# A one-core trunk layer: the feed-forward weights' sums moved in 64 long rows, loads issued one step before their use, and a rearranged last half

## The chip, the cores and the metric

The kernel runs on one core of a Trainium2 chip. The metric is the device time in microseconds, as the median of several runs. A profile shows one execution: PE is TensorE, ACT is ScalarE, DVE is VectorE, POOL is GpSimd, SP is SyncE, whose queue issues most of the DMAs.

## The reference

One layer of a streaming encoder, batch 1, 2048 frames, width 1024, 16 heads of 64, all in float32. x is the residual stream; g are gains.

```python
def rms_norm(x, g):
    return x * rsqrt(mean(x * x, axis=-1) + 1e-6) * g

# DEPTH = 1, mixer 0
h = rms_norm(x, g_pre_mix)
m = chunk_relpos_attention(h, w_qkv, w_o, rel_bias)
#   frame chunk c (64 frames) attends to chunks max(0, c-8)..c:
#   softmax(q k^T / 8 + bias[clipped relative position]) v, then @ w_o
x = x + rms_norm(m, g_post_mix)
h = rms_norm(x, g_pre_ffn)
x = x + rms_norm((silu(h @ w_gate) * (h @ w_up)) @ w_down, g_post_ffn)   # inner width 2816
```

## The kernel before

Activations lie transposed, features on the 128 partitions and frames along the rows, in halves of 512 frames; two halves are a group (`g` = 0, 1). Each float32 factor of a dense product is split into a high and a low part (`split`: ACT writes the high part, DVE the rest), and `products` issues three matmuls (high·high, high·low, low·high). One such triple of 512 columns is the unit of `tick`.

PE's order is written out by hand: `dense()` is a generator of PE's work, and the main loop takes pieces of it between the attention steps (`fill`). The instructions of the other engines are put in order by the tile framework's scheduler, which issues what its own model holds ready, by buffers and data; on the chip each engine then runs its list strictly in order. Work that lies beside the products waits in the list `later` as pairs of a cost and a step; `tick` adds the products done to a credit and runs the steps that it pays for. `pause(w)` is an empty step of cost w.

Attention runs first, for both groups. Each of 64 steps a group is: `scores` (PE products L555, DVE takes the bias and the maximum L564, ACT the exponential L568, POOL multiplies by the reciprocal of the sums L572), then `transposed` (PE transposes of the scores L588 and L599, DVE and ACT copy them out L591, L593, L600), and once in four steps `output`. PE cannot transpose scores that POOL has not scaled.

The feed-forward products use a scheme of seven block products in place of eight. It needs four sums of weight blocks, S1 to S4, for each of 11 column blocks of the gate and up weights (512 KB a block) and of the down weights (256 KB): 22 units. [...] S2 adds S1, and S4 adds S2. [...] The sums' tiles hold the column block in the middle, `[128, 11, 1024]`, so a transfer has 128 rows of 4 KB or 2 KB. The kernel asks for a small area for the descriptors of POOL's DMAs:

```python
    nc = bacc.Bacc("TRN2", target_bir_lowering=False, num_devices=1, dynamic_dma_scratch_size=512)
```

Buffers that matter here: `io` has 3 buffers of 512 columns; `narrow` takes turns over 9 (4 of the tag `sc`, 5 of `tmp` once the feed-forward phase has begun); `big` is one buffer of 10 × 512 columns, used by `Blocks.first` for the third columns' sources and then by `gate_up` for its terms (`p1`, `p5`, `u2`).

`Blocks` makes the normalised and combined columns of the feed-forward input: `sums` (squares), `spreads` (roots to rows), `column` (load and normalise), `first`, `second`, `third` for group 0 and `all` for group 1. `Late` is the norm and residual addition of a half whose product was left in DRAM: `sums`, `rstd`, `write`. In group 0 of the gate and up products, `later` holds the two halves' `Late` of group 1's attention, then `blocks[1].sums`. `gate_up` ends a block product in `closing` (DVE L980, ACT's sigmoid-linear unit L982).

The last stage is `down` for group 1. Its last product goes in two halves of 256 columns; `keep` stores a part (DVE L1075), squares it (ACT L243) and adds the squares (DVE L244). `rstd_steps` brings the squares' sum to PE (L258), takes mean and power on DVE and POOL (L260, L262), transposes the roots to rows (PE L274) and copies them out (ACT L275). `finish` multiplies (L1375), adds the residual (L1376) and stores, all additions on DVE; pieces of two columns for the first 256 frames, of four for the second. `Post.finish` does the same for the other half of the group and gives half of its additions to POOL (L392).

Of the kernel before, what the change touches and what calls it, by code (L numbers as in the profile page):

```python
# [50 lines left out]
def trunk(  # L51
# [45 lines left out]
    sum_gu = {n: dram.tile([P, NF // 2, 1024], F32, name=f"gu_{n}") for n in ("S1", "S2", "S3", "S4")}  # L97
    sum_d = {n: dram.tile([P, NF // 2, HALF], F32, name=f"d_{n}") for n in ("S1", "S2", "S3", "S4")}
# [114 lines left out]

    def pause(w):
        return [(w, lambda: None)]
# [30 lines left out]
    def rstd_steps(total, dst, wait=8.0, keep=None, bank=None):  # L246
# [8 lines left out]
        def by_token():  # L255
            pt = bank("pssq")
            for b in range(nb):
                pe.matmul(pt[:, 0, b : b + 1], total[:, b * P : b * P + P], ones[:, 0:1], start=True, stop=True)  # L258
# [5 lines left out]
        return [(1.0, by_token)] + pause(wait) + [(1.0, lambda: spread(r[0], dst, bank))]  # L264
# [4 lines left out]
    def spread(r, dst, bank=norm_bank):  # L269

        pt = bank("prs")
        nb = dst.shape[-1] // P
        for b in range(nb):
            pe.transpose(pt[:, b, :], r[:, b : b + 1].to_broadcast([P, P]), ident)  # L274
        act.activation(dst, pt[:, :nb, :].rearrange("p b t -> p (b t)"), AF.Copy)  # L275
# [92 lines left out]
    class Post:  # L368
# [31 lines left out]
        def write(self, w=1.6):  # L400
            def one(dt):
                def go():
                    y = self.y[dt]
                    n = y.shape[-1]
                    io = xp.tile([P, HALF], F32, tag="io", name="res", bufs=3)[:, :n]
                    sp.dma_start(io, self.res[:, dt, :])
                    dve.scalar_tensor_tensor(
                        y, y, gt[:, self.gain, dt : dt + 1], self.total, op0=ALU.mult, op1=ALU.mult
                    )
                    dve.tensor_tensor(y, io, y, op=ALU.add)  # L410
                    sp.dma_start(self.dst[:, dt, :], y)

                return w, go

            return [one(dt) for dt in range(KT)]
# [308 lines left out]
    class Blocks:  # L724
# [9 lines left out]
        def sums(self, w):  # L734

            steps = []
            for t in range(2):
                def one(k, t=t):
                    if k == 0:
                        self.total = nrm_tile("total")  # L740
                    c = io("sum")
                    sp.dma_start(c, self.src[t][:, k, :])
                    add_square(c, self.total, k == 0)

                steps += [(w, lambda k=k, one=one: one(k)) for k in range(KT)]
# [13 lines left out]
        def column(self, dst, t, k):  # L759
            sp.dma_start(dst, self.src[t][:, k, :])  # L760
            dve.scalar_tensor_tensor(
# [8 lines left out]
        def first(self, w):  # L770
# [3 lines left out]
            def load(k):  # L774
# [3 lines left out]
                c[k] = [io("b11"), io("b12"), io("b22")]  # L778
                for dst, t, kk in zip(c[k], (0, 1, 1), (k, k, k + 4)):
                    self.column(dst, t, kk)  # L780
                self.column(self.wait[:, 4 + k, :], 0, k + 4)

            def sums(k):
                b11, b12, b22 = c[k]
# [9 lines left out]

            for k in range(4):
                steps += [(w, lambda k=k, f=f: f(k)) for f in (load, sums, put)]
            return steps

        def all(self, w):
# [3 lines left out]
            def load(k):  # L803
                c[k] = [io("b11"), io("b12"), io("b22"), narrow("b21")]
                for dst, t, kk in zip(c[k], (0, 1, 1, 0), (k, k, k + 4, k + 4)):
                    self.column(dst, t, kk)

            def one(k):
                b11, b12, b22, b21 = c[k]
# [22 lines left out]
        def second(self, w):  # L832
            def one(k, name, t):
                c = io("b2")
                self.column(c, t, k + 4)
                self.put(name, k, c)

            return [(w, lambda k=k, n=n, t=t: one(k, n, t)) for n, t in (("B21", 0), ("B22", 1)) for k in range(4)]
# [709 lines left out]
```

## Time and profile before

| what | value |
|---|---|
| median of 3 runs | 2446.33 us |
| runs | 2441.12, 2446.33, 2449.23 us |
| profiled execution | 2441.91 us |
| its span, first to last instruction | 2440.1 us |
| granted TensorE clock, mean | 0.996 |
| PE busy | 2399.6 us (98%) |
| DVE, ACT, POOL busy | 1468.8, 1030.7, 302.6 us |
| DMA moved | 488.41 MB, 200 GB/s on average |

The span is divided about so: attention with the projections to 1153 us, gate and up products of group 0 from there, then its down products, and the same for group 1 to the end. In a table of windows the columns are the stretch, its length, the busy time of each engine (with instructions), the granted clock, the busy share of the 16 DMA engines and GB/s. A row of waits gives who waited for whom, the sum, how often, and the longest. A row of the timeline gives start, duration, engine, line and operation, and in brackets the idle time before it and what ended it.

### The profile page before, as it was taken

Reading aid. Unit: us, or ns where it says so; the run is one execution under the profiler, and the core shown is the slowest. Engines: PE = TensorE matmul, PEld = TensorE weight load, DVE = VectorE, ACT = ScalarE, POOL = GpSimd, SP = SyncE. Lnnn points to the kernel's source line nnn. Section 1 sums busy time; section 2 is a strip of 40 time slices with the busy share of each in tenths; the row PEclk is TensorE's granted clock in tenths of the full one; section 3 lists DMA queues with packets and bytes.
Section 4 is the critical chain, followed back from the end, with each engine's and each line's share of the span. In section 5 each row is a group of like instructions: output and inputs, shape, how many; then the busy total and the mean of one; then the engine's idle time right before and its main releaser. Section 6 shows DMA issues by size and latency. Waiting matters only on the chain.

```text
span 2440.1 us, 34891 instructions
## 1 busy us (share of the span) xinstructions
PE 2399.6 (98%) x12554; PEld 1993.0 (82%) x12554; DVE 1468.8 (60%) x2569; ACT 1030.7 (42%) x1807; POOL 302.6 (12%) x379
## 2 busy tenths in 40 slices
PE   9999999999999999999999999999999999999997
PEld 8887878788888888878888788888888888888886
DVE  6555455767555554667566665577666655555577
ACT  5444334654344443545333333365443333334444
POOL 0233233201233332210000000000000000000001
PEclk9999999999999999999999999999999999999999
DMA  7689888757898975546476755377667655457654
GB/s 219 196 216 234 221 229 203 222 183 200 226 250 214 243 182 133 144 143 225 157 252 201 242 171 170 123 246 256 210 214 246 219 178 160 135 170 243 195 188 147
DMA packets 209884, 488.41 MB, mean 200 GB/s; under 512 B 25360, under 2 KB 27424, under 8 KB 208432
## 3 DMA queue, kind: packets, MB, share of 16 engines
q1 hardware_dynamic: 197040, 451.59, 58.3%
q0 software_dynamic: 12672, 34.61, 9.3%
q8 instruction: 99, 1.62, 0.3%
q14 instruction: 73, 0.60, 0.1%
HBM read 356.54 MB, written 148.42 MB: 207 GB/s over the span
## 4 chain that ended last, share of the span: by engine, by line
PE 48%; DMA 4%; DVE 3%; issue 1%; ACT 0%; SPq 0%; DVEq 0%; ACTq 0%
PE pd L192 6%; PE pd L193 6%; PE pd L194 6%; PE pb L192 4%; PE pb L193 4%; PE pb L194 4%; PE pa L192 3%; PE pa L193 3%; PE pa L194 3%; PE pc L192 3%; PE pc L194 3%; PE pc L193 3%; DMA b<-x 1%; DMA res<-in_x 1%; DMA y<-y 1%
## 5 line engine op out<-in xcount | busy, mean ns | idle before, releaser
L568 ACT ACTIVATE sc<-sc,nmax 128x640 f32<-128x640 f32 (+4 forms) x256 | 193.1, 756 | 277.5 <-DVE nmax L564 276.7
L192 PE MATMUL mm<-hb,whi 128*128 128x512 f32 x704 | 290.0, 412 | 0.5 <-ACT y L239 0.5
L194 PE MATMUL mm<-hb,wlo 128*128 128x512 f32 x704 | 277.0, 393 | 0.0
L193 PE MATMUL mm<-hb,whi 128*128 128x512 f32 x704 | 276.1, 392 | 0.0
L572 POOL TENSOR_SCALAR sc<-sc,rows 128x640 f32<-128x640 f32 (+4 forms) x256 | 198.6, 813 | 438.4 <-DVE rows L571 418.7
L564 DVE CUSTOM_DVE_ANT_0 sc<-st,bias 128x640 f32<-128x640 f32 (+4 forms) x256 | 179.6, 738 | 100.2 <-PE st L556 94.9
L192 PE MATMUL pb<-hb,whi_gu_T 128*128 128x512 f32 x528 | 206.9, 392 | 4.8 <-DVE terms L980 4.8
L194 PE MATMUL pb<-hb,wlo_gu_T 128*128 128x512 f32 x528 | 206.0, 390 | 0.0
L193 PE MATMUL pb<-hb,whi_gu_T 128*128 128x512 f32 x528 | 205.9, 390 | 0.0
L262 POOL TENSOR_TENSOR rs<-ms,neg_half 128x4 f32<-128x4 f32 (+1 forms) x11 | 16.7, 1520 | 1248.1 <-DVE ms L260 1248.1
L192 PEld LDWEIGHTS mm<-hb,whi 128*128 128x128 f32 x704 | 132.9, 189 | 35.2 <-issue 14.7
L194 PEld LDWEIGHTS mm<-hb,wlo 128*128 128x128 f32 x704 | 132.4, 188 | 29.4
L193 PEld LDWEIGHTS mm<-hb,whi 128*128 128x128 f32 x704 | 133.1, 189 | 19.4
L193 PE MATMUL pd<-a,whi_d_T 128*128 128x512 f32 (+1 forms) x368 | 139.9, 380 | 0.4 <-DVE a L348 0.4
L192 PE MATMUL pd<-a,whi_d_T 128*128 128x512 f32 (+1 forms) x368 | 140.0, 381 | 0.0
L194 PE MATMUL pd<-a,wlo_d_T 128*128 128x512 f32 (+1 forms) x368 | 139.7, 380 | 0.0
L192 PE MATMUL pa<-hb,whi_gu_B 128*128 128x512 f32 x352 | 137.7, 391 | 0.5 <-ACT terms L961 0.5
L193 PE MATMUL pa<-hb,whi_gu_B 128*128 128x512 f32 x352 | 137.0, 389 | 0.0
L194 PE MATMUL pa<-hb,wlo_gu_B 128*128 128x512 f32 x352 | 137.0, 389 | 0.0
L192 PE MATMUL mm<-whi,hb 128*128 128x256 f32 x448 | 133.5, 298 | 0.0
L555 PE MATMUL st<-k,q 128*128 128x384 f32 (+1 forms) x448 | 131.9, 315 | 0.2 <-DVE nmax L564 0.2
L129 DVE TENSOR_TENSOR wlo_gu_T<-raw,whi_gu_T 128x1024 fp32r<-128x1024 f32 x88 | 107.4, 1221 | 40.5 <-ACT whi_gu_T L128 40.3
(219 smaller groups left out, 5642.8 us busy)
## 6 DMA issues: line engine op xcount, KB each, us to landing
raw<-gu_S SPq DMA_DIRECT2D x88, 512.0 KB, 3.9
raw<-in_w_gu SPq DMA_DIRECT2D x66, 512.0 KB, 4.1
q<-stage SPq DMA_DIRECT2D x128, 256.0 KB, 5.8
y<-y SPq DMA_DIRECT2D x96, 256.0 KB, 3.8
gu_S<-in_w_gu SPq DMA_DIRECT2D x44, 512.0 KB, 7.6
raw_a<-aT SPq DMA_DIRECT2D x88, 256.0 KB, 3.6
raw_d<-d_S SPq DMA_DIRECT2D x88, 256.0 KB, 3.6
raw<-in_w_a SPq DMA_DIRECT2D x42, 512.0 KB, 6.3
```

The source lines that it names most:

```text
L129: dve.tensor_tensor(lo, raw, hi.bitcast(F32), op=ALU.subtract)
L192: pe.matmul(pt, a_hi, b_hi, start=first, stop=False, skip_group_check=go_on)
L193: pe.matmul(pt, a_hi, b_lo, start=False, stop=False, skip_group_check=go_on)
L194: pe.matmul(pt, a_lo, b_hi, start=False, stop=last, skip_group_check=go_on)
L262: pool.tensor_tensor(r[0][:, :nb], m[:, :nb], neg_half.to_broadcast([P, nb]), op=ALU.pow)
L555: pe.matmul(st[:, a:b], q[:, 2 * h, cols], kk[:, h, key], start=True, stop=False)
L564: dve.tensor_tensor_reduce(out=sc[:, :n], in0=st[:, c0 : c0 + n], in1=rev, scale=-1.0, scalar=3.0e38, op0=ALU.add, op1=ALU.min, accum_out= ...
L568: act.activation(sc[:, :n], sc[:, :n], AF.Exp, bias=nmax, scale=-1.0, accum_out=rows[:, 0:1])
L572: last_pool[0] = pool.tensor_scalar(sc[:, :n], sc[:, :n], rows[:, 1:2], 1.0, op0=ALU.mult, op1=ALU.mult)
```

## The change

Five things are edited.

1. `weight_sums`: the sums' tiles and the down weights lie with the column block outermost, so that a block is contiguous; copies and adds are seen as 64 rows of twice the length (`long`, at most 8192 bytes a row). The order of the copies and adds over the steps is a new one: gate-and-up units and down units take turns, a unit's copies go out every second step, and its adds 4, 8, 10 and 14 steps after its first copy (before: 5, 6, 8, 11).
2. A helper `behind` makes steps in which the load of step k goes out with the use of step k − lag. `Post.write`, `Blocks.sums`, `Blocks.second`, `Late.sums` and `Late.write` use it; `Blocks.first` and `Blocks.all` issue their loads in a step of their own, ahead of the normalising (`norm`, now apart from `column`). `Late.write` holds `y` in a `narrow` buffer, and `first` and `second` take `io` and `narrow` buffers by turns.
3. `Blocks.third` of group 0 is run from `later` beside the first products, not ahead of them; the pause after it is 44 instead of 56, and one of 12 is put ahead of `blocks[1].sums`. The first `p1` pair of `gate_up` lies in `narrow` buffers.
4. In the last half the last column's squares stay in a tile of their own and go to PE as a second term of the sum; the roots' rows stay in PSUM and are read there by DVE; POOL makes one addition of the first 256 frames and two of the second; all pieces have two columns.
5. The pause ahead of the other half's norm is 6 instead of 4.

```diff
-    sum_gu = {n: dram.tile([P, NF // 2, 1024], F32, name=f"gu_{n}") for n in ("S1", "S2", "S3", "S4")}
-    sum_d = {n: dram.tile([P, NF // 2, HALF], F32, name=f"d_{n}") for n in ("S1", "S2", "S3", "S4")}
+    sum_gu = {n: dram.tile([NF // 2, P, 1024], F32, name=f"gu_{n}") for n in ("S1", "S2", "S3", "S4")}
+    sum_d = {n: dram.tile([NF // 2, P, HALF], F32, name=f"d_{n}") for n in ("S1", "S2", "S3", "S4")}
...
+    def behind(w, n, lag, load, use):
+        def one(k):
+            def go():
+                if k < n:
+                    load(k)
+                if k >= lag:
+                    use(k - lag)
+            return w * n / (n + lag), go
+        return [one(k) for k in range(n + lag)]
...
     def weight_sums():
+        def long(t):
+            return t.rearrange("(a b) c -> a (b c)", b=2)
         def copy(to, a):
             with tc.issue_after(last_sp[0].ins):
-                sp.dma_start(to, a)
+                last_sp[0] = nc.sync.dma_start(long(to), long(a), max_dma_last_dim=8192)
         def add(to, a):
             with tc.issue_after(last_pool[0].ins):
-                pool.dma_start(to, a, accum_op=ALU.add)
+                pool.dma_start(long(to), long(a), accum_op=ALU.add, max_dma_last_dim=8192)
         steps = [[] for _ in range(4 * len(units) + 8)]
         for u, (src, dst) in enumerate(units):
+            at = 8 * (u // 2) + u % 2
             for n, (to, a) in enumerate((("S1", "A21"), ("S3", "A11"), ("S2", "A11"), ("S4", "A12"))):
-                steps[4 * u + n].append((copy, dst[to], src[a]))
-            for n, to, a in ((5, "S1", src["A22"]), (6, "S3", src["A21"]), (8, "S2", dst["S1"]), (11, "S4", dst["S2"])):
-                steps[4 * u + n].append((add, dst[to], a))
+                steps[at + 2 * n].append((copy, dst[to], src[a]))
+            for n, to, a in ((2, "S1", src["A22"]), (4, "S2", dst["S1"]), (5, "S3", src["A21"]), (7, "S4", dst["S2"])):
+                steps[at + 2 * n].append((add, dst[to], a))
...
     class Late:
         def write(self, w):
-            def one(dt):
-                y, res = io("y"), io("res")
+            c = {}
+            def load(dt):
+                c[dt] = y, res = narrow("y"), io("res")
                 sp.dma_start(y, self.y[:, dt, :])
                 sp.dma_start(res, self.res[:, dt, :])
+            def use(dt):
+                y, res = c.pop(dt)
                 dve.scalar_tensor_tensor(
                     y, y, gt[:, self.gain, dt : dt + 1], self.total, op0=ALU.mult, op1=ALU.mult
                 )
                 dve.tensor_tensor(y, res, y, op=ALU.add)
                 sp.dma_start(self.dst[:, dt, :], y)
-            return [(w, lambda dt=dt: one(dt)) for dt in range(KT)]
+            return behind(w, KT, 1, load, use)
...
+            if (g, c) == (0, 0):
+                p1 = [narrow("p1") for _ in range(2)]
...
-        for step in blocks[0].third(0.0):
-            step[1]()
         for g in range(NG):
             i = 2 * g
             if g == 0:
-                later.extend(pause(56.0))
+                later.extend(blocks[0].third(1.5) + pause(44.0))
                 for t in range(2):
                     late = Late(y_d[t], POST_MIX, x[2 + t], x1_d[2 + t])
                     later.extend(late.sums(6.0) + late.rstd(6.0) + late.write(10.0))
-                later.extend(blocks[1].sums(8.0) + blocks[1].spreads())
+                later.extend(pause(12.0) + blocks[1].sums(8.0) + blocks[1].spreads())
...
             def keep(t, dt, here, put):
                 put(y[t][:, dt, here])
-                add_square(y[t][:, dt, here], total[t][:, here], t not in begun)
+                if t == 0 and dt == KT - 1:
+                    last_sq[here.start] = narrow("sq")[:, : here.stop - here.start]
+                    act.activation(last_sq[here.start], y[t][:, dt, here], AF.Square)
+                else:
+                    add_square(y[t][:, dt, here], total[t][:, here], t not in begun)
...
-            def finish(here, per):
+            def finish(r, here, n):
...
-                def one(k):
-                    a, b_ = (v[:, k : k + per, here] for v in (y[0], res[0]))
+                def one(k, eng):
+                    a, b_ = (v[:, k : k + 2, here] for v in (y[0], res[0]))
                     dve.tensor_tensor(a, a, r, op=ALU.mult)
-                    dve.tensor_tensor(b_, b_, a, op=ALU.add)
-                    sp.dma_start(out[i][:, k : k + per, here], b_)
-                return [(0.0, lambda k=k: one(k)) for k in range(0, KT, per)]
+                    eng.tensor_tensor(b_, b_, a, op=ALU.add)
+                    sp.dma_start(out[i][:, k : k + 2, here], b_)
+                return [lambda k=k: one(k, pool if k < KT - 2 * n else dve) for k in range(0, KT, 2)]
...
-                    later.extend(pause(4.0) + rstd_steps(post.total, post.total, 5.0) + post.finish(2.0, 2))
+                    later.extend(pause(6.0) + rstd_steps(post.total, post.total, 5.0) + post.finish(2.0, 2))
```

More of the change, by code (lines that the diff above doesn't have):

```diff
@@ L793, in put @@
                     self.put(name, k, src)
+            order = [(load, 0)]
             for k in range(4):
-                steps += [(w, lambda k=k, f=f: f(k)) for f in (load, sums, put)]
-            return steps
+                order += [(load, k + 1), (sums, k), (put, k)]
+            return steps + [(w, lambda k=k, f=f: f(k)) for f, k in order if k < 4]
         def all(self, w):
@@ L832, in second, with load, use @@
         def second(self, w):
[L833 to L838, printed above, removed]
+            c = {}
+            def load(n):
+                c[n] = (io, narrow)[n % 2]("b2")
+                self.column(c[n], n // 4, n % 4 + 4)
+            def use(n):
+                self.norm(c[n], n // 4, n % 4 + 4)
+                self.put(("B21", "B22")[n // 4], n % 4, c.pop(n))
+            return behind(w, 8, 2, load, use)
         def third(self, w):
@@ L1151, in one @@
                 sp.dma_start(self.dst[:, dt, :], y)
-            return [(w, lambda dt=dt: one(dt)) for dt in range(KT)]
+            return behind(w, KT, 1, load, use)
     def begin():
```

122 lines of the change are left out of this document (78 added, 44 removed).

## The prediction

> **What bounds the kernel now.** I read the page's busy times first: they say whether there is an engine whose work is the time, or waits.
>
> ```profile
> PE 2399.6 (98%) x12554; PEld 1993.0 (82%) x12554; DVE 1468.8 (60%) x2569; ACT 1030.7 (42%) x1807; POOL 302.6 (12%) x379
> ```
>
> TensorE is busy for 2399.6 of 2440.1 us. No part of the change takes a product away, so all it can win is the 40.5 us in which PE idles, and what PE loses at a lower clock. The windows say where the idle time lies (second column: PE busy; before the DMA share: granted clock), and PE's waits say who ends it (total, times, longest).
>
> ```profile
> 244.00:305.00 61.00, 56.53 (x387) 49.22 (x385) 27.66 (x76) 23.80 (x57) 17.54 (x24) 0.97 0.86 221
> 305.00:366.00 61.00, 55.20 (x295) 42.83 (x294) 31.13 (x76) 21.83 (x49) 20.59 (x27) 0.97 0.89 229
> 2379.00:2440.00 61.00, 47.28 (x255) 40.41 (x253) 43.17 (x71) 27.95 (x52) 10.08 (x5) 0.91 0.42 148
> ```
>
> ```profile
> PE tt L588 <- POOL sc L572: 8.2, 3, 4.7
> PE tt L599 <- DVE pT L591: 5.8, 8, 1.5
> PE pb L192 <- DVE terms L980: 4.8, 3, 3.1
> PE pssq L258 <- DVE total L244: 3.2, 3, 2.1
> PE pa L192 <- ACT terms L961: 0.5, 1, 0.5
> ```
>
> So 10.3 us of idle lie in 122 us of attention, 13.7 us in the last 61 us, and the rest is small. Three sites answer to three parts of the change.
>
> **Part 1, the weights' sums.** 88 adding transfers go out from POOL's queue (L868), one per score step, between the scalings of the scores (L572) for which PE waits. Look at one of them:
>
> ```profile
> q0 software_dynamic: 12672, 34.61, 9.3%
> 341.08 0.85 POOL L868 DMA_DIRECT2D gu_S<-gu_S  x1 [6.10 <-DVE nmax L564]
> 341.68 1.43 POOL L572 TENSOR_SCALAR sc<-sc,rows 128x384 f32<-128x384 f32 x2
> 351.36 0.87 POOL L868 DMA_DIRECT2D d_S<-d_S  x1 [8.25 <-issue]
> DMA to landing us min/median/max: 10.0/10.0/10.0
> 353.01 1.77 PE L588 MATMUL tt<-ident,sc 128*128 128x128 f32 x8 [4.66 <-POOL sc L572]
> POOL d_S L868 <- issue: 103.3, 28, 8.2
> POOL gu_S L868 <- issue: 47.7, 21, 6.8
> 268.22:271.63 3.41, 3.41 (x19) 3.41 (x18) 0.42 (x1) 0.43 (x1) 0.00 (x0) 0.50 0.86 245
> 353.55:356.96 3.41, 3.41 (x12) 2.81 (x11) 1.45 (x3) 1.11 (x2) 0.28 (x2) 0.50 0.51 79
> ```
>
> The landing line is that of the transfer issued at 341.08: it lands at 341.08 + 10.0 = 351.1. The next leaves POOL at 351.36, after 8.25 us in which POOL waited for nothing that the profile shows. Its data was not what it waited for: these two work on different tensors. The two scalings behind it on POOL wait with it, and PE waits 4.66 us for them. 49 issues waited in this way, 151 us in all. I read this as room for one transfer's packets and no more. 12672 packets over 88 transfers are 144 each, which is 16 × 9: on each of 16 DMA engines eight of a transfer's 128 rows and one more. With 64 rows it is 4 + 1 = 5. A room that holds nine and not eighteen holds two of five if it is ten or more; three if it is fifteen or more. Then POOL waits only for the transfer before the last, one score step earlier, and a landing of 10.0 us is covered by two steps (the two issues above are 10.3 us apart and were stretched by the wait itself).
>
> What goes: PE's 8.2 us, and the two half-clock stretches that follow the stalls (3.41 us each at 0.50, PE busy throughout: half of each is lost, 1.7 us, 3.4 together). **11.6 us.** Bounds: nothing, if the room was just nine or POOL sends adding transfers one by one; 13.5 us, if a third of the 5.8 us of L599 waits goes too. What is late next there is DVE's copy L591, which is in that row already. The longer order of copies and adds moves SP's 88 copies by up to three steps; each stays one a step, and the adds stay behind their copies by four steps or more (five before for the first, three between two adds, now four), so no wait for data is added. The weights' new order in memory leaves the SBUF loads at 128 rows: nothing.
>
> **Part 2, loads a step ahead.** The clearest site is where the first half's late norm ends and `blocks[1].sums` begins:
>
> ```profile
> 1361.82 5.35 DMA x<-y
> 1367.19 3.18 DMA sum<-x
> 1370.45 0.63 ACT L239 ACTIVATE total<-sum 128x512 f32<-128x512 f32 x1 [10.63 <-DMA sum<-x]
> 1377.55:1380.96 3.41, 2.94 (x7) 2.36 (x8) 3.06 (x5) 1.58 (x2) 0.00 (x0) 0.50 0.88 250
> DVE y L1147 <- DMA y<-y: 38.0, 19, 3.9
> ```
>
> The first two rows are of the chain that ended last (start, duration, what). The `sum` tile takes an `io` buffer that the last `y` held; it is free only when `y` is stored (5.35 us); then it is loaded (3.18 us); and ScalarE, in order, sits 10.63 us before the square of it, with the split of the next weights and the sigmoid of `terms` queued behind. PE pays the 3.1 us of the `pb` row and half of 2.94 us at clock 0.50, 1.5 us. With the change `y` lies in a `narrow` buffer, `res` alone takes one of three `io` buffers and frees it at DVE's addition, and a pause of 12 stands between: the wait on the store is gone, 4.6 us. The other 1.7 us of the `pb` row follow DVE's own waits for late `y` loads (38.0 us in all, 3.9 at most); a load one step of 10 × 8/9 = 8.9 credits ahead should cover 3.9 us, but these additions also stand in a queue of splits, so I take half, 0.8. **5.4 us**, bounds 0 and 6.3 (4.8 + 1.5).
>
> The same edit elsewhere (`Post.write`, `Blocks.first`, `all`, `second`, both `sums`) moves loads on SP's queue and the normalising on DVE's by one step, in stretches where PE has no wait in the rows above: cost nothing now, hidden by DVE's 40% idle time. If that cover fails, the price is one stall like the longest of PE's, 4.66 us, with 1.7 us of half clock. An SP load that now waits for a `narrow` buffer holds up the weights' loads queued behind it; those are asked for four products ahead, so that I expect no PE wait of it. For all the redrawn orders of DVE, ACT and SP together I take a loss of **2 us**, between 0 and one such stall, 6.4.
>
> **Part 3, small edits.** The third columns' splits move from in front of the first products to beside them, and the first `p1` pair lies outside the `big` buffer that these splits hold: the 0.5 us of the `pa` row goes; bounds 0 and 0.5, and −1 for two splits too many on ACT in front of a copy. A pause of 6 instead of 4 ahead of the second-last norm: of the `pssq` row all but the longest is 1.1 us; half goes. Together **1.0 us**.
>
> **Part 4, the end.**
>
> ```profile
> 2426.53 0.60 DVE hb L1375
> 2427.12 0.35 DVE total L244
> 2427.61 0.59 PE pssq L258 x4
> 2428.53 1.07 POOL L262 TENSOR_TENSOR rs<-ms,neg_half 128x2 f32<-128x2 f32 x1 [6.35 <-DVE ms L260]
> 2430.39 0.38 ACT L275 ACTIVATE total<-prs 128x256 f32<-128x256 f32 x1 [2.87 <-PE prs L274]
> 2428.45 1.20 DVE hb L1375 x2
> 2429.65 1.21 DVE hb L1376 x2
> 2430.86 2.31 DVE hb L1375 x2
> 2433.16 1.14 DVE hb L1376
> out_dram<-hb SPq DMA_DIRECT2D x6, 512.0 KB, 3.0
> out_dram<-hb SPq DMA_DIRECT2D x4, 256.0 KB, 2.2
> L392 POOL TENSOR_TENSOR hb<-hb,hb x4: 1285/2212/5346, 2375.4 to 2390.8; 128x512 f32<-128x512 f32 x4
> L389 DVE SCALAR_TENSOR_TENSOR hb<-hb,gt,total x8: 739/742/1789, 2371.3 to 2385.3; 128x512 f32<-128x512 f32 x8
> ```
>
> DVE works without a break from the first half's multiplications to the end, and the second half's roots arrive (2430.39 + 0.38) just as it gets free, so both must shrink. Roots: the last square goes to PE as a second term: L244 (0.35 and a hop, 0.45 us) goes, two more products of 0.15 us each come behind the square; the copy L275 and its hop (0.45) go, since DVE reads the bank: 0.45 − 0.3 + 0.45 = 0.6 us earlier. DVE: of what stands in front of the second half one addition (0.6) goes to POOL and one L244 (0.35) goes altogether, 0.95 us, so DVE is free by then. Second half: 4 multiplications and 2 additions at 0.6 us are 3.6 us, against 2.31 + 2 × 1.14 = 4.6 now; that is if POOL's two additions cost DVE nothing. If POOL and DVE shut each other out, 3.6 + 2 × 1.285 = 6.2. The L389 row has a median near its minimum and one at 1.789: most operations beside POOL's ran unslowed, so I stay nearer the lower bound, at 4.4: 0.2 us won. The last transfer is 256 KB instead of 512 KB: 0.8. **1.6 us**, bounds −0.2 (6.2) and 2.4 (3.6).
>
> [...] The 1.789 us row agrees with an exclusion; no row here shows a PSUM input beside POOL.
>
> **Sum.** 11.6 + 5.4 + 1.0 + 1.6 − 2 = 17.6 us off the profiled execution's 2441.9 us (span 2440.1). The median of the runs, 2446.33, is 4.4 us above that execution; taken off the median, the time is 2428.7 us.
>
> **Rivals.**
> (a) POOL still sends one at a time (the room is nine, or it is no matter of room). For it: in no place do two overlap, so the trace can't tell these apart. Against: nothing but the code's halved rows. Then 11.6 us stay: 17.6 − 11.6 = 6.0, 2440.3 us.
> (b) The loads come no earlier, because SP issues them when a buffer is free and not when the step says so. For it: the 5.35 us store in front of the `sum` load is a buffer's wait. Against: the change also moves `y` to other buffers. 12.2 us, 2434.1.
> (c) Slower: the long rows make DMA the bound in attention. Place: 127 to 427 us, where the sums run.
>
> ```profile
> 127.00:427.00 300.00, 289.52 (x1865) 243.93 (x1865) 152.85 (x387) 118.92 (x273) 93.94 (x127) 0.99 0.88 222
> raw<-in_w_o SPq DMA_DIRECT2D x20, 512.0 KB, 5.3
> raw<-in_w_o SPq DMA_DIRECT2D x6, 1024.0 KB, 4.9
> ```
>
> The share of the 16 engines there is 0.88. POOL's 9.3% of the span is 227 us of all engines, and nearly half of its transfers (41 of 88 would be 106 us) fall in these 300 us, a share of 0.35. It decides once these packets take over a third more time per byte (0.35 × 0.34 = 0.12). At twice the time the share would be 1.23 and the stretch 69 us longer; with the 6.0 us of the other parts, 2446.3 + 69 − 6 = 2509 us; at a half more, 0.88 + 0.175 = 1.055, 16 us and 2456 us. Against it: a row twice as long (1024 KB over 128 rows) lands in 4.9 us where the shorter takes 5.3.
> (d) At the end POOL and DVE exclude each other throughout (6.2 us instead of 4.4), and the pow of the second roots stands behind a POOL addition of 1.285 us: 17.6 − 1.8 − 1.3 = 14.5, 2431.8 us. For it the 5346 ns of one L392 row; against it the three shorter ones.
>
> **How the numbers follow.** The forecast as it stands 0.50; (a) 0.18; (b) 0.11; (c) 0.05; (d) 0.11; some other new stall that eats most of the gain 0.05. About 0.3% (7.3 us) is what a measurement here can tell from no change: the runs before spread over 2441.12 to 2449.23. So faster means under 2439.0: the forecast, (b), (d) and four tenths of (a), 0.79; same: the rest of (a) and most of the other stall, 0.15; slower: (c) and the rest, 0.06. The likeliest case's own range is 2421 (13.5 + 6.3 + 1.6 + 2.4 = 23.8 with no loss, 2422.5, and somewhat less for the runs' spread) to 2435 (the loss of 6.4 in full, and a little). The range over the cases is 2420 to 2443: (a) with the spread of a run, and not (c).
>
> **What would show it.** Part 1: POOL's waits put down to "issue" fall from 151 us to under 20, two transfers overlap, the `tt L588` row falls under 2 us, and no half-clock stretch is left near 268 or 353 us; if POOL's issues still follow a landing by 0.3 us, (a) holds. Part 2: no ACT row with 10 us of idle time before `total<-sum`; the `pb` row under 2 us; `y L1147 <- DMA y<-y` far below 38 us, else (b). Part 4: from the last product to the end of the span some 13 us instead of 14.6; L392-like POOL rows over 2 us, or DVE additions over 1 us, speak for (d). DMA share above 0.95 with longer landings of the weights speaks for (c). The prediction is wrong as a whole if PE's idle time stays near 40 us, or if it falls and matmuls get longer.

## The result, and the profile after

The changed kernel takes 2416.16 us (median of 4, 2415.36 to 2416.70) against 2443.72 us (2441.12 to 2449.23) for the kernel before in the same comparison: a ratio of 0.9878, interval 0.9854 to 0.9902. The forecast, 2428.7, had the right sign and about two thirds of the size (17.6 us off the median, 27.6 measured); the time lies below its range. The profiled execution takes 2415.77 us (span 2414.0, clock 0.998), 26.1 us less than the one before, where the prediction's sum was 17.6.

Busy time of the engines and POOL's DMA queue, from the page of the changed kernel:

```profile
PE 2392.5 (99%) x12562; PEld 1991.0 (82%) x12562; DVE 1462.7 (61%) x2568; ACT 1031.3 (43%) x1805; POOL 294.7 (12%) x382
q0 software_dynamic: 5632, 34.61, 8.7%
```

PE's idle time went from 40.5 to 21.5 us (span less busy), and its busy time fell by 7.1 us although it multiplies the same matrices. The queue moves the same 34.61 MB in 5632 packets instead of 12672. That is 64 a transfer on average, where the prediction reckoned 16 × 5 = 80 for all of them: 44 × 16 × 5 and 44 × 16 × 3 make the 5632. In the trace the queue's packets are 4224 of 8192 bytes and 16 of 4 bytes a transfer: only the 512 KB blocks go as 64 rows, the 256 KB blocks as 32, three packets an engine with the small one. The first two windows shown before, the last 61 us of the span, and the waits of PE (a choice of rows):

```profile
244.00:305.00 61.00, 61.00 (x421) 53.26 (x420) 28.79 (x79) 24.94 (x59) 18.77 (x27) 1.00 0.94 262
305.00:366.00 61.00, 61.00 (x388) 51.41 (x386) 34.08 (x92) 26.11 (x60) 20.38 (x30) 1.00 0.94 245
2353.00:2414.00 61.00, 49.25 (x269) 42.45 (x268) 44.84 (x71) 27.24 (x51) 14.45 (x9) 0.94 0.45 156
```

```profile
PE po L645 <- DVE pT L619: 1.6, 1, 1.6
PE tt L627 <- DVE pT L619: 1.0, 3, 0.3
PE pssq L275 <- ACT sq L1428: 0.9, 1, 0.9
PE pb L192 <- DVE terms L1036: 0.2, 1, 0.2
```

In these two windows of attention PE is busy throughout and at full clock, with the DMA share up from 0.86 and 0.89 to 0.94. Score transposes waiting for POOL's scalings, 8.2 us before, have no row left; those waiting for DVE's copies (L627, before L599) fell from 5.8 to 1.0 over the whole span, and `pb` from 4.8 to 0.2.

To see where the 26.1 us went, I cut both profiles at the same PE instructions: group 0's attention, its gate and up products, its down products, and from the last product to the end. Before, then after:

```profile
57.13:477.74 420.61, 406.55 (x2513) 337.45 (x2512) 228.97 (x580) 180.51 (x411) 122.46 (x167) 0.99 0.82 218
1146.65:1578.14 431.49, 427.20 (x1897) 352.64 (x1896) 266.30 (x354) 157.97 (x215) 5.36 (x4) 1.00 0.60 189
1578.14:1787.64 209.50, 209.50 (x926) 173.31 (x925) 144.47 (x226) 107.51 (x189) 0.00 (x0) 1.00 0.71 233
2425.53:2440.13 14.60, 1.27 (x6) 0.81 (x6) 9.67 (x15) 1.31 (x3) 1.07 (x1) 0.61 0.41 144
```

```profile
56.58:460.46 403.88, 401.11 (x2513) 334.95 (x2512) 223.55 (x580) 180.61 (x411) 117.08 (x167) 1.00 0.83 225
1129.77:1554.26 424.49, 424.49 (x1897) 351.92 (x1896) 266.10 (x353) 157.37 (x214) 5.74 (x4) 1.00 0.59 189
1554.26:1764.98 210.72, 210.06 (x926) 173.29 (x924) 144.32 (x226) 108.03 (x190) 0.00 (x0) 1.00 0.70 231
2401.16:2413.99 12.83, 1.52 (x11) 1.10 (x10) 8.18 (x14) 0.92 (x2) 4.84 (x4) 0.70 0.48 163
```

The same number of matmuls stands in each product stage, so the lengths can be set against each other: attention −16.7 us, gate and up −7.0, down +1.2, the end −1.8. All other stages together (first loads, the two projections after attention, group 1) give the remaining −1.9, of which no one is over 1.0. So nearly everything comes from two places.

**Attention.** POOL's issues no longer wait. POOL's row of waits, its timeline, and the landing of the first transfer in it:

```profile
POOL d_S L921 <- issue: 0.4, 1, 0.4
361.98 0.78 POOL L921 DMA_DIRECT2D d_S<-d_S  x1
364.82 0.74 POOL L600 TENSOR_SCALAR sc<-sc,rows 128x128 f32<-128x128 f32 x2 [2.06 <-DVE rows L599]
365.51 0.81 POOL L921 DMA_DIRECT2D gu_S<-in_w_gu  x1
d_S<-d_S POOLq DMA_DIRECT2D x1, 256.0 KB, 7.8
```

The first lands at 361.98 + 7.8 = 369.8; the second has left POOL at 365.51. Two are under way at once: 38 of the 88 transfers leave before the one ahead of them has landed, none did before, and 151 us of issue waits have become 0.4.

**Gate and up.** The square of the first `sum` tile and DVE's waits for `y`:

```profile
1349.48 0.63 ACT L253 ACTIVATE total<-sum 128x512 f32<-128x512 f32 x1 [3.75 <-DMA sum<-x]
DVE y L1212 <- DMA y<-y: 21.4, 12, 3.4
```

ScalarE waits 3.75 us for it instead of 10.63, and PE not at all: 424.49 us busy of 424.49.

### The profile page after: what moved, and what is told of

The parts are those of the page before. It is cut to its first block, busy times and chain, and to the rows that moved or that the text cites. A ratio compares the mean times of both kernels' runs of the same rounds, so it can differ in the third digit from the quotient of the medians.

```text
span 2414.0 us, 34849 instructions
## 1 busy us (share of the span) xinstructions
PE 2392.5 (99%) x12562; PEld 1991.0 (82%) x12562; DVE 1462.7 (61%) x2568; ACT 1031.3 (43%) x1805; POOL 294.7 (12%) x382
## 3 DMA queue, kind: packets, MB, share of 16 engines
q0 software_dynamic: 5632, 34.61, 8.7%
## 4 chain that ended last, share of the span: by engine, by line
PE 54%; DMA 1%; DVE 1%; issue 0%; ACT 0%; SPq 0%; POOL 0%; DVEq 0%; ACTq 0%
PE pd L193 6%; PE pd L192 6%; PE pd L194 6%; PE pb L192 5%; PE pb L193 5%; PE pb L194 5%; PE pa L192 3%; PE pc L192 3%; PE pa L193 3%; PE pc L193 3%; PE pc L194 3%; PE pa L194 3%; PE mm L192 1%; PE mm L194 1%; PE mm L193 1%; DMA y<-y 1%
## 5 line engine op out<-in xcount | busy, mean ns | idle before, releaser
L600 POOL TENSOR_SCALAR sc<-sc,rows 128x640 f32<-128x640 f32 (+4 forms) x256 | 191.6, 751 | 652.0 <-DVE rows L599 598.1
```

Source lines behind the costliest of these rows:

```text
L600: last_pool[0] = pool.tensor_scalar(sc[:, :n], sc[:, :n], rows[:, 1:2], 1.0, op0=ALU.mult, op1=ALU.mult)
```

## The experiments

Times are medians with lowest, highest and number of runs; the ratio to the kernel before, run beside it on the same chip, has its interval. "Issue waits" are POOL's rows of waits put down to "issue"; stage lengths come from one profile each.

### The weights' sums: rows, order or room

The theory: POOL's descriptors have room for one transfer of 128 rows and not for two. The rivals: the new order is what frees POOL, or less time per byte in the DMA engines.

`e1_sums_only`: the kernel before with the layout and `weight_sums` of the diff and nothing else.

> Before, with the weights' sums alone as after (64 long rows and the new order; loads, third columns and end as before). If the sums carry the whole gain of the first group's attention (16.7 us between the two profiles, where the prediction had 11.6), the profiled time is 2441.9 - 17 = 2425 us, and the first group's attention takes 404 us instead of 421. If part of the 16.7 us comes from the other edits, less: 2430 us (the 11.6 us of the prediction).

2428.99 us (2425.38 to 2436.23, 7), ratio 0.9942 [0.9923, 0.9962]. Group 0's attention:

```profile
57.04:460.06 403.02, 401.21 (x2514) 335.08 (x2513) 223.33 (x580) 180.81 (x411) 117.26 (x167) 1.00 0.83 226
```

The whole gain of that stage is there: 17.6 us less than before.

`e2_rows_only`: the long rows, with the tiles' layout that they need, in the order of before (an excerpt; the copies change likewise).

```diff
+        def long(t):
+            return t.rearrange("(a b) c -> a (b c)", b=2)
...
-                pool.dma_start(to, a, accum_op=ALU.add)
+                pool.dma_start(long(to), long(a), accum_op=ALU.add, max_dma_last_dim=8192)
```

> Before, with the long rows (64 a transfer) in the old order. Theory of the room (POOL's queue holds one transfer of 128 rows, several of 64): POOL's waits put down to issue fall from 151 us to under 20, time 2426 us. Theory of the order (the longer distance between the steps frees POOL, the rows do nothing): waits stay near 150 us, time 2441 us.

2431.59 us (2427.65 to 2434.59), 0.9946 [0.9928, 0.9964]; attention 404.43 us, issue waits 0.5. The rows alone do it.

`e3_order_only`: the new order, in the rows of before (an excerpt; the adds change likewise).

```diff
-                steps[4 * u + n].append((copy, dst[to], src[a]))
+                steps[at + 2 * n].append((copy, dst[to], src[a]))
```

> Before, with the new order of copies and adds but transfers of 128 rows as before. Theory of the room: POOL still issues each transfer 0.31 us after the landing of the one before, waits near 150 us, time 2442 us. Theory of the order: waits under 20 us, 2426 us.

2448.07 us (2442.29 to 2455.04, 10), 1.0013 [0.9996, 1.0029]. Its attention stage and POOL's waits:

```profile
56.74:484.64 427.90, 409.66 (x2513) 336.68 (x2512) 231.92 (x580) 181.34 (x411) 123.08 (x167) 0.99 0.80 213
POOL d_S L868 <- issue: 103.4, 23, 8.7
POOL gu_S L868 <- issue: 50.6, 18, 6.2
```

No gain, and 154 us of waits as before: the order is not it. The stage is even 7.3 us longer than before's in this profile, which the time does not confirm.

`e4_room_640`: the kernel before with a larger descriptor area. Every engine's list of instructions is that of before; rows, packets and order stay.

```diff
-dynamic_dma_scratch_size=512
+dynamic_dma_scratch_size=640
```

> Before, with one number changed: the area for the descriptors of POOL's DMAs is 640 bytes instead of 512; every engine has the same instructions in the same order. Theory of the room, with 512 bytes just short of two transfers of 128 rows: two fit in 640, waits fall under 20 us and the time is 2426 us with no other change. If a transfer needs more than half of 640, or POOL sends adding transfers one by one whatever the room: waits stay near 151 us, 2442 us.

2429.30 us (2428.61 to 2435.45), 0.9946 [0.9927, 0.9965]. Its stage, POOL's issues, and PE's longest wait in the stage:

```profile
56.96:460.97 404.01, 401.43 (x2514) 335.02 (x2513) 224.27 (x580) 180.35 (x411) 120.33 (x167) 1.00 0.85 226
POOL d_S L868 <- issue: 1.1, 3, 0.8
PE tt L599 <- DVE pT L591: 1.2, 2, 0.7
```

This is the decisive one. The packets are still the short ones, 12672 of them at 9.0% of the span (9.3% before), and 16.6 us of the stage go all the same. It was the room, and long rows are one way to make do with it.

`e10_room_192`: the changed kernel with less room, so that two of the 512 KB transfers do not fit either.

```diff
-dynamic_dma_scratch_size=512
+dynamic_dma_scratch_size=192
```

> After, with the area for the descriptors of POOL's DMAs at 192 bytes instead of 512; the same instructions in the same order. From before at 512 (one transfer of 9 packets an engine, not two) and at 640 (two) a packet takes between 512/18 = 28.4 and 640/18 = 35.6 bytes. 192 bytes then hold 5.4 to 6.8 packets: one gate-and-up transfer (5) and not one of each kind (5 + 3). Theory of the room: POOL waits for each landing again, 100 to 150 us put down to issue, and the first group's attention is 10 to 17 us longer, 2426 to 2433 us. If short rows were slow for another reason, no difference, 2416 us.

2427.68 us (2426.80 to 2432.67), 0.9929 [0.9914, 0.9945].

```profile
55.96:471.80 415.84, 405.39 (x2513) 335.75 (x2512) 228.62 (x580) 181.09 (x411) 119.06 (x167) 1.00 0.81 219
POOL d_S L921 <- issue: 91.9, 23, 8.8
POOL gu_S L921 <- issue: 55.6, 19, 5.7
```

The waits are back, 147.5 us in 42 issues, and 12.0 us of the 16.7. Only one pair of the 88 transfers ran together in this profile, two of 256 KB; the landing is that of the first:

```profile
165.27 0.79 POOL L921 DMA_DIRECT2D d_S<-d_S  x1 [8.79 <-issue]
166.71 1.07 POOL L921 DMA_DIRECT2D d_S<-in_w_d  x1
DMA to landing us min/median/max: 6.4/6.4/6.4
```

The first lands at 171.7, the second has left at 166.71. So three and three packets fit into 192 bytes, at most 32 bytes a packet if all take the same.

The size of a transfer is an estimate from the runs alone. POOL's issue waits (151 us with 512 bytes, 1.1 us with 640 in `e4`) say that two transfers of nine packets an engine do not fit into 512 bytes and do fit into 640. Then nine packets take over 256 and at most 320 bytes, 28.4 to 35.6 a packet, and at most 32 by the pair above.

`e5_all_but_sums`: the changed kernel with the old sums (rows and order).

> After, with the weights' sums as before (128 rows, old order; the weights lie as after). If the parts add up, this saves what the sums alone do not: 26.1 - 16.7 = 9.4 us, so 2432.5 us in the profile, the first group's attention back at 421 us, POOL's issue waits back near 150 us. The executions of before spread over 8 to 12 us and those of after over 1.3 us: if the loads a step ahead remove the spread, these executions lie within 3 us of each other; if the sums remove it, they spread over 8 us.

2429.88 us (2427.42 to 2444.46, 8), 0.9957 [0.9936, 0.9978]; attention 419.78 us with 149 us of issue waits; gate and up products:

```profile
1143.90:1568.40 424.50, 424.50 (x1898) 352.16 (x1896) 266.07 (x353) 157.39 (x214) 5.74 (x4) 1.00 0.58 189
```

So the two places do not depend on each other: without the sums' part the 7.0 us are still won. The sums are worth 13.7 us between the medians (2429.88 − 2416.16); these runs spread over 17 us, so the loads alone do not bring the narrow spread of the changed kernel.

`e15_old_order`: the changed kernel, long rows, old order.

> After, with the old order of copies and adds (long rows stay). With the sums alone the new order was 2.6 us faster in the median (2429.0 against 2431.6), less than these executions spread. If the order is worth that, 2418.8 us; if not, 2416.5 us.

2414.67 us (2413.78 to 2416.18), 0.9875 [0.9858, 0.9891]. The new order shows no gain.

### The loads: the step ahead or the buffer

`e6_late_old`: the changed kernel with the old `Late` and the old pauses (an excerpt; `sums` of `Late` goes back likewise).

```diff
-                c[dt] = y, res = narrow("y"), io("res")
+                y, res = io("y"), io("res")     # load and use in one step
-                later.extend(blocks[0].third(1.5) + pause(44.0))
+                later.extend(blocks[0].third(1.5) + pause(56.0))
-                later.extend(pause(12.0) + blocks[1].sums(8.0) + blocks[1].spreads())
+                later.extend(blocks[1].sums(8.0) + blocks[1].spreads())
```

> After, with the late norm of group 0 and 1 as before: loads in the step of their use, both tiles in io buffers, and the pauses 56 and none instead of 44 and 12. If these loads carry the gain of the first gate-and-up products (7.0 us between the profiles), the wait of 3 us in front of the closing of the terms is back with a half-clock stretch, 2415.8 + 5 to 7 = 2421 to 2423 us, and the spread of the executions grows to several us. If the gain there came from the third columns or the p1 pair, 2416 us.

2426.80 us (2420.04 to 2429.02), 0.9923 [0.9900, 0.9946]:

```profile
1132.84:1564.25 431.41, 426.99 (x1897) 353.09 (x1896) 265.12 (x352) 156.84 (x212) 4.43 (x4) 1.00 0.57 185
1358.64 0.63 ACT L1038 ACTIVATE terms<-terms 128x512 f32<-128x512 f32 x1 [6.63 <-DVE terms L1036]
1359.73 0.63 ACT L253 ACTIVATE total<-sum 128x512 f32<-128x512 f32 x1 [0.46 <-DMA sum<-x]
```

The length of before to 0.1 us. All of the second gain sits in this class and its pauses. But the one long wait of before is not there: ScalarE waits 0.46 us for the `sum` load, and 6.63 us for DVE's closing ahead of it.

`e14_late_old_new_pauses`: the same, but with the pauses of the change.

> After, with the old late norm (loads in the step of use, both tiles in io) but the new pauses of 44 and 12. If the pause ahead of the next sums is what takes away the wait of ACT for the stored tile, the first gate-and-up products take 424 to 427 us and the time is 2417 to 2419 us; if buffers and loads do it, it is as with the old pauses: 2424 to 2427 us and executions 5 to 9 us apart.

2427.79 us (2425.51 to 2435.36), 0.9932 [0.9911, 0.9953]:

```profile
1130.46:1566.39 435.93, 428.81 (x1897) 354.42 (x1896) 264.87 (x352) 156.51 (x212) 5.74 (x4) 0.99 0.58 183
1355.33 0.63 ACT L253 ACTIVATE total<-sum 128x512 f32<-128x512 f32 x1 [9.59 <-DMA sum<-x]
DVE y L1203 <- DMA y<-y: 41.2, 20, 4.1
```

The pauses win nothing: with them ScalarE waits 9.59 us for the load behind the store. Which wait is the long one, this or that of `e6`, changes from one profile to the other; the stage is as long as before or longer in both.

`e13_late_same_step`: the changed kernel with `y` in a `narrow` buffer, but each load in the step of its use. The line is edited in `sums` and in `write` of `Late`, so that, other than the expectation says, the late sums do not load a step ahead either.

```diff
-            return behind(w, KT, 1, load, use)
+            return [(w, lambda dt=dt: (load(dt), use(dt))) for dt in range(KT)]
```

> After, with the late norm's write loading in the step of its use; y stays in a narrow buffer, the late sums load a step ahead and the pauses are as after. If the buffers and not the step decide when a load goes out (rival b of the prediction), no difference: 2416.5 us, gate-and-up products of group 0 in 424.5 us. If the step ahead is what counts, up to half of the 10.6 us by which the old late norm was slower comes back: 2419 to 2422 us.

2416.10 us (2414.24 to 2416.92), 0.9878 [0.9863, 0.9892]:

```profile
1129.99:1554.51 424.52, 424.52 (x1897) 351.84 (x1896) 265.50 (x353) 157.62 (x214) 5.74 (x4) 1.00 0.59 189
DVE y L1212 <- DMA y<-y: 13.7, 10, 2.4
```

That is the changed kernel. From `e14`, on the same chip, it differs by the buffer of `y` alone: 11.7 us, and DVE's waits for `y` fall from 41.2 us to 13.7, lower even than the 21.4 with loads a step ahead. Issuing the load of this class a step earlier is worth nothing; that `y` no longer holds an `io` buffer until its store is done is worth everything that this class wins.

### The small edits and the end

`e8_third_in_front`: the changed kernel with the third columns' splits ahead of the products, the first `p1` pair in `big` and the one pause of 56, as before.

```diff
-                p1 = [narrow("p1") for _ in range(2)]
...
+        for step in blocks[0].third(0.0):
+            step[1]()
...
```

> After, with the third columns' splits ahead of the first products again and the first p1 pair in the big buffer. By the prediction 0.5 us slower, 2416.3 us, with PE waiting 0.5 us for ACT's copy of the first terms. If the splits beside the products cost as much as they save, no difference.

2414.34 us (2413.22 to 2420.15), 0.9882 [0.9860, 0.9903]; gate and up 424.49 us, the same as the changed kernel, and group 0's down products 209.51 instead of 210.72. The edit gains nothing; the 1.2 us that the change loses in that stage are not there without it, in one profile.

`e7_end_old`: the changed kernel with the end of before (only the pause of 6 stays).

> After, with the last half as before (squares all added on DVE, roots copied to SBUF, all additions on DVE, pieces of four columns in the second part). By the prediction 1.6 us slower; by the two profiles (from the last product to the end 12.8 us instead of 14.6) 1.8 us: 2417.6 us. If POOL's additions cost what they save: 2416 us or less.

2416.91 us (2416.22 to 2417.91), 0.9889 [0.9867, 0.9910]. From the last product to the end:

```profile
2399.89:2414.46 14.57, 1.01 (x6) 0.71 (x6) 9.63 (x15) 1.31 (x3) 1.07 (x1) 0.68 0.41 144
```

14.57 us against 12.83: the end is worth 1.7 us in the profile, 0.8 between the medians, which the intervals do not tell apart.

`e9_end_adds_on_dve`: the changed kernel with all additions of the end on DVE.

```diff
-                return [lambda k=k: one(k, pool if k < KT - 2 * n else dve) for k in range(0, KT, 2)]
+                return [lambda k=k: one(k, dve) for k in range(0, KT, 2)]
```

> After, with POOL's three additions of the last half given back to DVE. In the profile of after the second half's last operations take 4.79 us with two additions on POOL; eight of 0.6 us on DVE alone are 4.8. So no difference, 2416 us. If POOL's share is what shortens the end, 1.2 us slower.

2417.17 us (2415.30 to 2418.51), 0.9881 [0.9865, 0.9898]:

```profile
2402.00:2415.63 13.63, 1.77 (x10) 1.20 (x10) 9.23 (x17) 0.92 (x2) 1.07 (x1) 0.63 0.44 154
```

0.8 us longer in the profile; in the time it can't be seen.

`e11_third_in_front_one_add`: `e8` with one of POOL's two additions of the second half given back to DVE.

```diff
-                    for step in finish(rows_[1], second, 2):
+                    for step in finish(rows_[1], second, 3):
```

> After, with the third columns in front and the first p1 pair in the big buffer (that run measured 2414.3 us), and in the second half one addition on POOL instead of two. POOL's addition of 1.34 us then runs beside the four multiplications and no DVE addition meets it: 7 x 0.6 = 4.2 us instead of 4.79, 0.6 us less. 2413.7 us, 2.5 us under after if the 1.8 us of the third columns' run are real, 0.6 us if not.

2415.47 us (2414.60 to 2416.11), 0.9875 [0.9860, 0.9890]. The second half takes 5.0 us on DVE, because an addition of the first half now falls into it: no gain.

### Putting it together

`e12_after_again`: the changed kernel once more, beside e9 to e11.

> After itself, unchanged, on the same chip as the others of this call, to read differences of 1 to 2 us: 2416 us, within 2 us from run to run.

2417.15 us (2414.70 to 2418.13), 0.9881 [0.9866, 0.9895], beside a kernel before of 2447.11 us (2442.91 to 2452.70, 7).

`e16_room_and_buffer`: the kernel before with two edits of one word each.

```diff
-dynamic_dma_scratch_size=512
+dynamic_dma_scratch_size=640
-                y, res = io("y"), io("res")
+                y, res = narrow("y"), io("res")
```

> Before, with two edits of one word each: the descriptors' area at 640 bytes and y of the late norm in a narrow buffer; rows, order, steps, third columns and end as before. If room and buffer are all of the gain but the end's 1.8 us: 2416.2 + 1.8 = 2418 us, executions within 4 us of each other. If the other edits hold a share, 2421 us or more.

2421.39 us (2414.96 to 2427.24, 6), 0.9916 [0.9899, 0.9934]; attention 404.24 us, gate and up 426.01. Two words bring 21 of the 28 to 30 us by which the changed kernel is below before. In the profiled execution (2417.72 us) only 1.95 us are missing to the changed kernel, 1.7 of them from the last product to the end (14.57 us against 12.83). In the median 5.2 us are missing (7.1 against `e17`, run beside it). Which of the other edits holds them, and why this kernel still spreads over 12 us, is not settled.

`e17_without_idle_parts`: the changed kernel without the edits that gained nothing (third columns as in `e8`, old order as in `e15`).

> After, without the edits that showed no gain of their own: old order of the sums (rows long), third columns in front, first p1 pair in the big buffer. Both alone measured 2414.3 and 2414.7 us, after itself 2416.2 and 2417.2. If their gains are real and add up: 2413 us; if they are what the executions spread: 2414 to 2416 us.

2414.33 us (2411.28 to 2414.61), 0.9882 [0.9868, 0.9897]. The lowest median of all, but not told apart from the changed kernel by the ratio: leaving those edits out shows no cost.

## Why the prediction was wrong

The forecast missed by 12.5 us. 8.5 of them are the sum (26.1 in the profile against 17.6), 4.0 the subtraction from the median. The step that failed first is the price of the stall in Part 1, with 5.1 of the 8.5 us; the loss of 2 us that was taken off, and the offset of the median, come behind it.

**The chain of the argument held.** PE was the bound, only its idle and half-clock time could be won, and the two places named gave 23.7 of the 26.1 us. Rivals (a) and (c) fell: POOL overlaps its transfers, and PE is busy throughout in the windows with a DMA share of 0.94. (d) fell too: the second half takes 4.8 us and not 6.2 (Part 4).

**Part 1 was mis-sized: 11.6 us, 16.7 measured** (16.6 with the room alone). The cause was right, POOL's room, and `e4` and `e10` show it from both sides. But I charged the stall with PE's waits for POOL and two half-clock stretches alone, and took the rest of the stage's waits for the next thing late. In part they were consequences of the same stall. Before, in group 0's attention, PE also waited 3.5 us for DVE's copies:

```profile
PE tt L599 <- DVE pT L591: 3.5, 4, 1.5
```

In `e4`, where nothing but the room differs, 1.2 are left, and 0 in the changed kernel. With the row `po`, which waits for the same copies, it is 2.8 to 4.3 us in the profiles with the stall (before, `e3`, `e5`, `e10`) and 0.6 to 2.3 without it (the changed kernel, `e1`, `e2`, `e4`, `e15`, `e16`). The timeline of before shows one way from a late POOL to a late DVE, beside the landing of the transfer that POOL had issued at 232.30 and the group row of the same DVE operation:

```profile
239.83 0.85 POOL L868 DMA_DIRECT2D gu_S<-in_w_gu  x1 [5.29 <-DVE t L492]
240.43 1.86 POOL L572 TENSOR_SCALAR sc<-sc,rows 128x640 f32<-128x640 f32 x2
240.45 2.92 DVE L129 TENSOR_TENSOR wlo<-raw,whi 128x1024 fp32r<-128x1024 f32 x1 [0.66 <-ACT whi L128]
DMA to landing us min/median/max: 7.2/7.2/7.2
L129 DVE TENSOR_TENSOR wlo<-raw,whi 128x1024 fp32r<-128x1024 f32 x78 | 98.8, 1267 | 35.4 <-ACT whi L128 33.3 <-PE tt L599 1.9
```

The bracket names DVE for the 5.29 us in front of the transfer, but the one before it landed at 232.30 + 7.2 = 239.5, and this one left 0.3 us later, as behind an "issue" wait: the rows put down to "issue" do not hold all of the stall. The transfer left late, the scalings behind it fell on DVE's split, and that took 2.92 us where one takes 1.27 on average: longer by nearly the 1.86 us of POOL's work beside it. That this is how all of the 3.5 us arose is only argued. The upper bound, 13.5 us, was too low in any case. Of the 5.1 us that the term missed, 3.1 are idle time (11.3 us went, of 8.2), 2.7 of them the waits for DVE's copies. The other 2.0 are busy time of PE (5.4 went, of 3.4); `e10` has 4.3 us more of it than the changed kernel, and the cause stays open.

**Part 2: the size was near, one step was wrong.** 5.4 us for the loads, and 0.5 of Part 3 in the same stage; 7.0 measured, 4.3 of it idle time and 2.7 busy time of PE. The 4.6 us were set down to the buffer of `y`, and the buffer is what wins (`e13` against `e14`); but they were read from one wait, the store in front of `sum`, and `e6` loses the whole 7.0 us without that wait. The 0.8 us for a load one step ahead failed: in `e13` it goes out in the step of its use and nothing is lost. That the sum came near is in part luck. Rival (b)'s mechanism is shown, loads go out when a buffer is free (before, the `sum` load at 1367.19, as the store that held its buffer landed, 1361.82 + 5.35); it fell because the change frees the buffer too.

**The loss of 2 us for redrawn orders did not come**, save for 1.2 us in group 0's down products and 0.75 in the projection after attention; the other stages gained as much and more. With the 0.5 us that Part 3 was to give outside the gate and up stage, this accounts for 2.2 us of the miss.

**Part 3: 1.0 us.** The third columns and `p1` gained nothing (`e8`, which has no `pa` row in that stage either). The longer pause was not tried alone; the `pssq` wait of 0.8 us in group 1's down products has no row any more.

**Part 4: 1.6 us, 1.8 measured, put together otherwise; that it came so near is luck.** The timeline of the end, DVE and then POOL:

```profile
2405.14 0.69 DVE L1444 TENSOR_TENSOR hb<-hb,prs 128x512 f32<-128x512 f32 x1 [0.49 <-PE prs L302]
2405.74 0.68 DVE L1445 TENSOR_TENSOR hb<-hb,hb 128x512 f32<-128x512 f32 x1
2406.34 1.88 DVE L1444 TENSOR_TENSOR hb<-hb,prs 128x512 f32<-128x512 f32 x3
2408.14 1.79 DVE L1445 TENSOR_TENSOR hb<-hb,hb 128x512 f32<-128x512 f32 x2
2405.90 2.87 POOL L1445 TENSOR_TENSOR hb<-hb,hb 128x512 f32<-128x512 f32 x2 [1.29 <-DVE hb L1444]
```

The roots came earlier by more than thought: from the last product to the second half's first multiplication 3.98 us instead of 5.27, 1.3 won where 0.6 stood. The second half itself won nothing: 2405.14 to 2409.93 is 4.8 us, against 4.6 before and 4.4 forecast, since the pair of additions behind POOL's took 1.79 us instead of about 1.2. No run shows the 4.4 us: the second half takes 4.9 us with all additions on DVE (`e9`, 2407.20 to 2412.08) and 5.0 in `e11`. The stretch after DVE's last operation fell by 0.64 (forecast 0.8): 1.3 − 0.2 + 0.6 is the 1.8. Here the trace can show what it could not before: three multiplications with rows from PSUM took 1.88 us beside POOL's additions, and two in `e9`, with none on POOL, 1.28: 0.6 us for each one more in both. Of the pair of additions, which read SBUF alone (1.28 us in `e9`), the first took 1.19 us and ended 0.56 after POOL's two (2408.77). That it waited for POOL's end is only argued.

**The median.** The profiled execution before lay 4.4 us below the median of its runs, and I carried that offset over. The changed kernel's runs lie within 1.3 us (3.4 in `e12`) and its profiled one 0.4 below the median. The offset belonged to the kernel before, whose 18 runs went from 2441.04 to 2452.88 us beside `e1` to `e4`; their median, 2444.14, lies only 2.2 above the profiled execution, so that about half of the offset was the chance of three runs. What narrows the spread is not shown: with one stall left it was 17 us (`e5`), 9 us (`e6`) and 6 us (`e10`), but 12 us in `e16`, where both fixes are in.

## What to carry to other kernels

A wait put down to "issue" in front of a DMA, ending just after the last one landed, was a queue without room here (151 us of such waits, 1.1 with the larger area of `e4`): try a larger descriptor area before changing rows or order. When a stall is in the middle of a pipeline, count the smaller waits of the same stage and the time that PE is busy longer there as its consequences, at least for the upper bound (here 2.7 and 2.0 of the 5.1 us that the term missed). When a load is late, ask what holds its buffer before moving its issue. And do not carry the distance from median to profile, read from three runs, over to another kernel: here it went from 4.4 us to 0.4.

## What the runs showed of the hardware

With 512 bytes of descriptor area no transfer of nine packets per engine left before the one ahead of it had landed, and POOL's issues waited 151 us; with 640 bytes they waited 1.1 us (`e4`). By these two runs such a transfer takes over 256 and at most 320 bytes, an estimate. The scalings behind a waiting transfer in POOL's list came late with it: PE's waits for them were 8.2 us before and have no row in the changed kernel. On an engine that is 12% busy these waits cost 16.6 us of a stage and about 13 us of the kernel's time (`e4`: 12.7 between the profiled executions, 14.8 between the medians). Making the rows longer did not make the transfers faster to a degree that matters: the queue's share went from 9.3% to 8.7% of the span, and is 9.2% in `e10` with the same rows.
